# The plain split inputs of two feed-forwards begin at other bytes of on-chip memory

## The chip, the cores and the metric

The program runs on one NeuronCore of a Trainium2 chip. The metric is the device time of one execution in microseconds (us), the median of several. All arrays are float32.

## The reference

Four sub-layers over 256 tokens of width 2048: a gated DeltaNet mixer, a feed-forward, an HGRN2 mixer, a feed-forward. Each begins with an RMS norm and ends with a residual addition.

```python
def swiglu(h, w_gate, w_up, w_down):
    return (jax.nn.silu(h @ w_gate) * (h @ w_up)) @ w_down
...
    h = x
    for layer in range(DEPTH):            # DEPTH = 2
        if layer % 2 == 0:
            h = h + gdn_mixer(rmsnorm(h, gdn_norm[j]), gdn_w_in[j], ...)
        else:
            h = h + hgrn2_mixer(rmsnorm(h, hgrn_norm[j]), hgrn_w_in[j], ...)
        h = h + swiglu(rmsnorm(h, ffn_norm[layer]), w_gate[layer], w_up[layer], w_down[layer])
    return rmsnorm(h, final_norm)
```

The hidden width of a feed-forward is 5632, 22 groups of 256 (`N_FF`).

## The kernel before

**Split products.** A float32 operand is split into a high half (what TensorE's `float32r` form keeps) and a low half (the rest). A product is three matmuls: high by high, high by low, low by high. The input of a sub-layer is kept transposed, 128 features on the partitions and 256 tokens along the row, as `xt_h` (high) and `xt_l` (low): four tiles each, 4 blocks of 128 features in a tile, 1,024 bytes a block and partition. Weights come from memory as `raw` (or `sraw`), 1,024 columns at a time; ScalarE writes their high half `wh`, VectorE the low half `wl`.

**Two kinds of matmul.** A matmul has a stationary operand of 128 columns, loaded ahead by a weight load, and a moving one that streams past it. In the mixers' query, key and forget projections the weights are stationary and `xt` moves, 256 columns (`mm_cols`). Everywhere else (`mm_rows`) `xt`, or `ht` or `ot` of the output products, is stationary and the weights move, 512 columns; in the profile such a matmul reads `main<-wh,xt_h`: the moving operand stands first, the stationary one second.

**The feed-forward.** Of the 11 pairs of groups in each, four (`FF_PLAN`: those ahead of a colon) are computed by a seven-product scheme for 2 by 2 block matrices (`mixed_group`). Its products take 256 moving columns and write to `aux`. For products 1, 2 and 4 the stationary operand is a plain half of `xt`; for 3, 5, 6 and 7 it is a sum of blocks of the input, made once per feed-forward by `mix_inputs` into `mixh` and `mixl`. One step of a mixed group is four items: 6 matmuls of product 1; 12 of products 2 and 3 in turn; 12 of 5 and 7; 12 of 6 and 4. There are 4 such steps in a group, 8 mixed groups in a feed-forward. `among` puts the items between items of plain groups, or of the output product (`down`), 12 matmuls of 512 columns each. The other groups are plain: `xt` stationary, 512 moving columns.

**Where operands begin.** Tiles are laid out in the order of their pools. Some have columns to spare (`PAD`), and `make` picks where the data begins. All bytes here are modulo 512, within a partition. Moving weights begin at byte 32, stationary weights (in `mm_cols`) at 108 (`wh`) and 364 (`wl`). `mixh` begins at 108 and `mixl` at 364 (19 columns past 32 and 288). The eight `xt` tiles, `ht` and `ot` begin at 32. Every block of 128 columns is 512 bytes, so all blocks of an operand begin at the same byte modulo 512.

**The order.** The kernel records all operations and a planner then puts them in order, by costs and due times (`Recorder.plan`); matmuls of the main stream keep the order in which they were written. The next sub-layer's `xt` is made by `make_xt`, called by `next_input` for each quarter of the output product as that is finished.

Of the kernel before, what the change touches and what calls it, by code (L numbers as in the profile page):

```python
# [9 lines left out]
F32R = mybir.dt.float32r  # L10
# [7 lines left out]
P = 128  # L18
T = 256
# [60 lines left out]


PAD = 64
IN_COLS = {"wh": 108, "wl": 364}


class Op:
    __slots__ = ("eng", "method", "args", "kw", "cost", "lag", "main", "pred", "succ", "n", "late", "call", "tiles", "heirs", "share")

    def __init__(self, eng, method, args, kw, cost=0.0, lag=0.0, main=False):
        self.eng, self.method, self.args, self.kw = eng, method, args, kw  # L90
        self.cost, self.lag, self.main = cost, lag, main
        self.pred, self.succ = {}, []
        self.call, self.tiles, self.heirs = None, [], []
        self.share = 1.0


class Virtual:


    def __init__(self, pool, shape, dt, tag, bufs, name, stream=False):  # L100
        self.pool, self.shape, self.dt, self.tag, self.bufs, self.name = pool, list(shape), dt, tag, bufs, name
        self.stream = stream
        self.pad = self.cols = 0
        self.row = int(np.prod(shape[1:]))
        self.nbytes = self.row * (1 if dt == U8 else 4)
        self.touched = []
        self.before, self.ordered = None, False
        self.left = 0
        self.free = 0.0
        self.together = [self]  # L110
        self.slot = self.real = None
# [43 lines left out]
class Recorder:  # L155
# [38 lines left out]

    def after(self, ap):

        self.wanted = [other for other, *_ in self.virtual(ap).touched]

    def together(self, *aps):
        group = [self.virtual(ap) for ap in aps]  # L200
# [251 lines left out]
    def make(self, v):  # L452
        shape = [v.shape[0], v.shape[1] + v.pad] if v.pad else v.shape
        v.real = v.pool.real.tile(shape, v.dt, tag=f"{v.tag}.{v.slot}", name=v.name)
        assert v.real.offset == 0
        if v.pad:
            n = v.pool.padded.setdefault((v.tag, v.slot), len(v.pool.padded))
            at = 32 + n * v.pad * 4 % 512
            want = IN_COLS[v.tag] if v.cols else 32 + n % 2 * 512
            v.skip = (want - at) // 4  # L460
            assert 0 <= v.skip <= v.pad
# [61 lines left out]
class Trunk:  # L523
# [40 lines left out]
    def opening(self, items, setup):  # L564
        first = items[0].begin

        def begin():
            setup()
            first()

        items[0].begin = begin
        return items
# [3 lines left out]
    def setup(self):  # L576
        nc, c = self.nc, self.const
        t = lambda shape, tag, dt=F32: self.tile(c, shape, tag, dt)
        self.x_home = self.tile(self.dram, [T, D], "x_home", bufs=1)
        self.x_at, self.x = self.a["x"], {}  # L580
        neghalf = t([P, 72], "neghalf")
        self.neghalf = neghalf[:, 0:8]
        self.rstd = t([P, 2], "rstd")
        self.rstdh = t([P, 2], "rstdh")
        self.ssp = t([P, 2, 4], "ssp")
        self.ss = t([P, 2], "ss")
        head = t([P, P + 64], "head")
        nc.sync.dma_start(head, self.a["head"])
        nc.ops[-1].lag = 2.4
        self.queue = [nc.ops[-1]]  # L590
        self.ident = head[:, 0:P]
        self.norms = head[:, P : P + 64].rearrange("p (n c) -> p n c", n=4)
        self.ones = t([P, P], "ones")
        nc.gpsimd.memset(self.ones, 1.0)
        self.rstd_row = t([P, T], "rstd_row")
        self.junk = t([P, 512], "junk")
        self.vjunk = t([P, 320], "vjunk")[:, 0:256]
        nc.gpsimd.memset(self.neghalf, -0.5)
        self.xt_h = [t([P, 4, T], f"xt_h{i}", F32R) for i in range(4)]
        self.xt_l = [t([P, 4, T], f"xt_l{i}", F32R) for i in range(4)]  # L600

    def start(self, norm, row):

# [25 lines left out]
    def stream(self, items):  # L629
# [3 lines left out]
        def place(tag, cols):  # L633
            w = self.tile(self.wsplit, [P, 1024], tag, F32R, ordered=True)
            v = nc.virtual(w)
            v.pad, v.cols = PAD, cols
            return w
# [154 lines left out]
        if cg == 3:  # L792
            self.x_at = self.x_home

    def next_input(self, norm, row):


        def after(cg):
            self.make_xt(cg, norm)
            self.sumsq(cg)  # L800
            if cg == 3:
                self.make_rstd(row)

        return after
# [27 lines left out]
    def mix_inputs(self):  # L832
# [6 lines left out]
        self.mixed = [[], [], [], []]  # L839
        both = [self.tile(self.pool, [P, 4096 + PAD], f"mix{x}", F32R)[:, 19 : 19 + 4096] for x in "hl"]  # L840
        row = self.rstd_row.unsqueeze(1).broadcast_to([P, 4, T])
        for q in range(2):
# [16 lines left out]
            for n in range(4):  # L859
# [6 lines left out]
                self.mixed[n].append((h, low))  # L866

    def ffn(self, j, after):
        nc, a = self.nc, self.a
        hts, h1s, quick = {}, {}, {}  # L870
# [172 lines left out]
        def down(part, cg, pairs):  # L1043
            w = a[f"ffn_d{j}_{part}"]
            lo = sum(FF_PARTS[:part]) // 2

            def operand(kt):
                h, l = hts[pairs[kt // 4]]
                return h[:, kt % 4, :], l[:, kt % 4, :]

            last = part == len(FF_PARTS) - 1
            apart = last and j == 1 and cg == 3

            def end(ps):
                if apart:
                    self.finish_last(ps)
                    return
                self.add_x(ps, cg, not (last and j == 1))
                if last:
                    after(cg)  # L1060

            mm = self.mm_apart if apart else self.mm_rows
            n = len(pairs)
            return self.group(
                [w[cg, p - lo] for p in pairs],
                lambda ps, i, h, l: mm(ps, i, h, l, n, operand), end,
                lambda: self.load_x(cg), apart,
            )
# [425 lines left out]
    def gdn_o(self, hg, st):  # L1494
# [37 lines left out]
        st["ot"] = self.head_out(o, st["zs"], scale, self.gdn_hn)  # L1532

    def gdn(self, after):
        a = self.a
        states = [{} for _ in range(N_HG)]
# [41 lines left out]
    def out_proj(self, name, p, states, last, after):  # L1578
        two = states[2 * p : 2 * p + 2]

        def begin(cg):
            self.load_x(cg)

        def operand(kt):
            h, l = two[kt // 4]["ot"]
            return h[:, kt % 4, :], l[:, kt % 4, :]

        def make(cg):
            def end(ps):
                self.add_x(ps, cg)  # L1590
                if last:
                    after(cg)

            return self.group(
                [self.a[name][p, cg, i] for i in range(2)],
                lambda ps, i, h, l: self.mm_rows(ps, i, h, l, 2, operand), end,
                lambda: begin(cg),
            )

        return [item for cg in range(4) for item in make(cg)]  # L1600
# [260 lines left out]
    def finish(self, cg):  # L1861
        nc = self.nc
        if cg == 0:
            self.last = self.tile(self.pool, [P, 4096 + PAD], "mixl", F32R, ordered=True).bitcast(F32)[:, 0:D]
            nc.gpsimd.dma_start(self.last, self.a["final_norm"].broadcast_to([P, D]))
            self.y = self.tile(self.pool, [P, 4096 + PAD], "mixh", F32R, ordered=True).bitcast(F32)[:, 0:4096].rearrange("p (t c) -> p t c", t=2)
            self.part = self.tile(self.pool, [P, 2], "part")
# [43 lines left out]
    def run(self):  # L1911
        self.setup()
        self.start(0, True)
        items = self.gdn(self.next_input(1, True))
        items += self.ffn(0, self.next_input(2, True))
        items += self.hgrn(self.next_input(3, True))
        items += self.ffn(1, self.finish)
        self.stream(items)
        self.leave()
# [91 lines left out]
```

## Time and profile before

| | us |
|---|---|
| time before, median of 3 (lowest to highest) | 2740.96 (2739.41 to 2741.87) |
| profiled execution, its own time | 2739.51 |
| its span, first to last instruction | 2737.7 |
| DeltaNet mixer, about | 0 to 824 |
| first feed-forward, about | 824 to 1534 |
| HGRN2 mixer, about | 1534 to 2020 |
| second feed-forward, about | 2020 to 2727 |

PE is TensorE's matmuls, PEld its weight loads, DVE VectorE, ACT ScalarE. All instructions are issued from one helper line, so groups are told apart by the names of their tiles and by their sizes. The listed duration of a matmul contains its way through the array and overlaps the next one; the time from one start to the next tells what a matmul costs in a stream.

### The profile page before, as it was taken

The numbers are of one execution on the slowest core, as the hardware profiler recorded it, in microseconds if no ns is written. First come the engines' busy times: TensorE is split into PE (matmuls) and PEld (weight loads), VectorE is DVE, ScalarE is ACT, GpSimd is POOL, SyncE is SP. The second block draws the span as 40 slices with busy tenths as digits, with TensorE's granted clock in tenths as the row PEclk, the third lists the DMA queues.
The fourth block names the chain that finished last, engine by engine and source line by source line (L and its number), as shares of the span: only waits on it lengthen the run. The fifth ranks groups of instructions, "written<-read, shape, count | busy, mean of one in ns | idle before, by whom it ended". The sixth has DMA issues, their size and how long they took to land.

```text
span 2737.7 us, 44285 instructions
## 1 busy us (share of the span) xinstructions
PE 2719.8 (99%) x16822; PEld 2355.8 (86%) x16822; DVE 2168.5 (79%) x3309; ACT 1549.2 (57%) x2192; POOL 307.6 (11%) x466
## 2 busy tenths in 40 slices
PE   9999999999999999999999999999999999999998
PEld 9888888888888888888888989988888888888887
DVE  7787888877768898889867688778678898888665
ACT  6646666565555555555545556556465555555543
POOL 1213222232110000000010100000100000000000
PEclk9999999999999999999999999999999999999999
DMA  7686568686676667766676755545676667666764
GB/s 262 202 282 224 183 217 279 215 277 220 220 252 224 219 212 245 238 216 216 228 235 217 228 167 182 170 166 179 224 264 212 217 223 239 223 230 221 250 209 167
DMA packets 170376, 605.92 MB, mean 221 GB/s; under 512 B 21675, under 2 KB 22843, under 8 KB 170033
## 3 DMA queue, kind: packets, MB, share of 16 engines
q1 hardware_dynamic: 138912, 503.15, 56.1%
q0 software_dynamic: 30960, 99.08, 11.3%
q8 instruction: 132, 2.16, 0.3%
q14 instruction: 84, 0.68, 0.1%
q10 hardware_dynamic: 288, 0.85, 0.1%
HBM read 563.10 MB, written 39.89 MB: 220 GB/s over the span
## 4 chain that ended last, share of the span: by engine, by line
PE 96%; DVE 2%; ACT 1%; issue 1%; POOLq 0%; POOL 0%; DVEq 0%; ACTq 0%
PE main L496 80%; PE aux L496 17%; DVE wl L496 1%; DVE turned L496 1%; ACT wh L496 0%; ACT dec L496 0%; DVE htl L496 0%; DVE sraw L496 0%; ACT xt_h L496 0%; DVE h L496 0%; DVE utmp L496 0%; DVE pre L496 0%; DVE u L496 0%; ACT mixh L496 0%; POOLq L2007 0%
## 5 line engine op out<-in xcount | busy, mean ns | idle before, releaser
L496 ACT ACTIVATE wh<-raw 128x1024 fp32r<-128x1024 f32 x817 | 864.9, 1060 | 934.5 <-PE main L496 826.2
L496 DVE TENSOR_TENSOR wl<-raw,wh 128x1024 fp32r<-128x1024 f32 x817 | 1002.6, 1229 | 422.3 <-ACT wh L496 412.3
L496 PE MATMUL main<-wh,xt_h 128*128 128x512 f32 x1664 | 651.5, 391 | 0.8 <-ACT wh L496 0.8
L496 PE MATMUL main<-wl,xt_h 128*128 128x512 f32 x1664 | 650.7, 391 | 1.3 <-DVE wl L496 1.3
L496 PE MATMUL main<-wh,xt_l 128*128 128x512 f32 x1664 | 650.3, 391 | 0.0
L496 PEld LDWEIGHTS main<-wh,xt_l 128*128 128x128 f32 x1664 | 312.5, 188 | 65.1
L496 PEld LDWEIGHTS main<-wh,xt_h 128*128 128x128 f32 x1664 | 312.7, 188 | 62.8 <-ACT wh L496 1.2
L496 PEld LDWEIGHTS main<-wl,xt_h 128*128 128x128 f32 x1664 | 312.6, 188 | 61.7 <-DVE wl L496 1.6
L496 ACT ACTIVATE wh<-sraw 128x1024 fp32r<-128x1024 f32 (+1 forms) x256 | 243.4, 951 | 136.7 <-PE main L496 96.3
L496 DVE TENSOR_TENSOR wl<-sraw,wh 128x1024 fp32r<-128x1024 f32 (+1 forms) x256 | 278.3, 1087 | 27.1 <-ACT wh L496 25.0
L496 PE MATMUL main<-xt_h,wh 128*128 128x256 f32 (+1 forms) x1040 | 288.7, 278 | 0.7 <-ACT wh L496 0.7
L496 PE MATMUL main<-xt_h,wl 128*128 128x256 f32 (+1 forms) x1040 | 288.3, 277 | 1.1 <-DVE wl L496 0.9
L496 PE MATMUL main<-xt_l,wh 128*128 128x256 f32 (+1 forms) x1040 | 288.2, 277 | 0.3 <-DVE xt_l L496 0.3
L496 PE MATMUL main<-wh,hth 128*128 128x512 f32 x680 | 266.5, 392 | 1.0 <-ACT hth L496 1.0
L496 PE MATMUL main<-wl,hth 128*128 128x512 f32 x680 | 266.2, 391 | 0.0
L496 PE MATMUL main<-wh,htl 128*128 128x512 f32 x680 | 265.2, 390 | 0.4
L496 PEld LDWEIGHTS main<-xt_h,wl 128*128 128x128 f32 (+1 forms) x1040 | 194.4, 187 | 1.6 <-DVE wl L496 1.5
L496 PEld LDWEIGHTS main<-xt_h,wh 128*128 128x128 f32 (+1 forms) x1040 | 194.5, 187 | 1.3 <-ACT wh L496 0.9
L496 PEld LDWEIGHTS main<-xt_l,wh 128*128 128x128 f32 (+1 forms) x1040 | 194.5, 187 | 1.0 <-DVE xt_l L496 0.5
L496 PEld LDWEIGHTS main<-wh,htl 128*128 128x128 f32 x680 | 127.7, 188 | 29.2 <-DVE htl L496 1.7
L496 PE MATMUL main<-wh,ot_l 128*128 128x512 f32 x384 | 151.3, 394 | 0.0
L496 PE MATMUL main<-wh,ot_h 128*128 128x512 f32 x384 | 150.5, 392 | 0.0
(238 smaller groups left out, 4078.5 us busy)
## 6 DMA issues: line engine op xcount, KB each, us to landing
raw<-in_ffn_gu SPq DMA_DIRECT2D x224, 512.0 KB, 4.7
raw<-in_ffn_d SPq DMA_DIRECT2D x176, 512.0 KB, 4.7
sraw<-in_ffn_gu SPq DMA_DIRECT2D x128, 512.0 KB, 5.2
raw<-in_hgrn_in SPq DMA_DIRECT2D x128, 512.0 KB, 4.1
raw<-in_gdn_kq SPq DMA_DIRECT2D x64, 512.0 KB, 5.3
raw<-in_gdn_v SPq DMA_DIRECT2D x64, 512.0 KB, 4.8
raw<-in_gdn_z SPq DMA_DIRECT2D x64, 512.0 KB, 4.9
raw<-in_gdn_out SPq DMA_DIRECT2D x64, 512.0 KB, 5.1
```

Source lines behind the costliest of these rows:

```text
L496: getattr(getattr(tc.nc, op.eng), op.method)(*args, **kw)
```

## The change

The four high tiles become one tile of 4,096 columns and 24 to spare, the four low ones one tile of 4,096 columns and 104 to spare. A new pair is declared ahead of each sub-layer (`new_xt`), in the same memory, with its own beginning: byte 32 for both halves in the mixers ("rows"), byte 108 (high) and 364 (low) in the feed-forwards ("mixed"). Together the tiles are 512 bytes longer than before, so that whatever lies behind them keeps its byte modulo 512. `after`, which orders the sums of squares behind the writes of one quarter, now looks at the quarter's region instead of at its tile. On every engine the instructions, their order and the places where they wait are the same as before; only addresses differ.

```diff
+XT_PAD = {"h": 24, "l": 104}
+XT_SKIP = {"rows": {"h": 0, "l": 104}, "mixed": {"h": 19, "l": 59}}
...
     def after(self, ap):
-        self.wanted = [other for other, *_ in self.virtual(ap).touched]
+        v = self.virtual(ap)
+        p0, p1, f0, f1 = v.region(ap)
+        self.wanted = [
+            other for other, _, (a0, a1, b0, b1) in v.touched if a0 < p1 and p0 < a1 and b0 < f1 and f0 < b1
+        ]
...
-        if v.pad:
+        if v.pad and v.skip is None:
...
-        self.xt_h = [t([P, 4, T], f"xt_h{i}", F32R) for i in range(4)]
-        self.xt_l = [t([P, 4, T], f"xt_l{i}", F32R) for i in range(4)]
+        self.new_xt("rows")
+
+    def new_xt(self, kind):
+        both = []
+        for half in "hl":
+            t = self.tile(self.const, [P, 16 * T], f"xt_{half}", F32R, ordered=True)
+            v = self.nc.virtual(t)
+            v.pad, v.skip = XT_PAD[half], XT_SKIP[kind][half]
+            t = t.rearrange("p (g k t) -> p g k t", g=4, k=4)
+            both.append([t[:, cg] for cg in range(4)])
+        self.xt_h, self.xt_l = both
...
-    def next_input(self, norm, row):
+    def next_input(self, norm, row, kind):
         def after(cg):
+            if cg == 0:
+                self.new_xt(kind)
             self.make_xt(cg, norm)
...
-        items = self.gdn(self.next_input(1, True))
-        items += self.ffn(0, self.next_input(2, True))
-        items += self.hgrn(self.next_input(3, True))
+        items = self.gdn(self.next_input(1, True, "mixed"))
+        items += self.ffn(0, self.next_input(2, True, "rows"))
+        items += self.hgrn(self.next_input(3, True, "mixed"))
```

More of the change, by code (lines that the diff above doesn't have):

```diff
@@ L103, in __init__ @@
         self.pad = self.cols = 0
+        self.skip = None
         self.row = int(np.prod(shape[1:]))
```

## The prediction

> **What bounds the kernel now.** I read the page first (the span, the engines' shares, the chain that ended last), then the windows of the two feed-forwards, the waits there, and last single matmuls in the timeline. From the page:
>
> ```profile
> span 2737.7 us, 44285 instructions
> PE 2719.8 (99%) x16822; PEld 2355.8 (86%) x16822; DVE 2168.5 (79%) x3309; ACT 1549.2 (57%) x2192; POOL 307.6 (11%) x466
> PE 96%; DVE 2%; ACT 1%; issue 1%; POOLq 0%; POOL 0%; DVEq 0%; ACTq 0%
> ```
>
> The chain is PE for 96% of the span. Next the two feed-forwards by windows (stretch, its length, then busy time and count of PE, PEld, DVE, ACT, POOL, granted clock, DMA share, GB/s), and PE's waits in the first of them:
>
> ```profile
> 823.70:1533.90 710.20, 709.50 (x3782) 611.96 (x3781) 580.35 (x749) 378.49 (x442) 40.19 (x65) 1.00 0.69 226
> 2019.90:2727.30 707.40, 706.69 (x3758) 609.44 (x3756) 576.86 (x742) 373.07 (x430) 38.36 (x63) 1.00 0.68 221
> PE main L496 <- ACT hth L496: 0.5, 2, 0.3
> ```
>
> PE is busy all but 0.7 us of each and waits 0.5 us in all of the first; DVE, the next fullest, is at 580 of 710. So a feed-forward lasts as long as its matmuls take from start to start, and a nanosecond off a matmul there is a nanosecond off the program until DVE, with 18% to spare, comes due. The granted clock is full.
>
> What the change touches is the stationary `xt` of the feed-forwards. How many matmuls that is, by the windows of `xt_h` and of `xt_l` alone (first the two of `xt_h`, then of `xt_l`), and the groups of 256 moving columns, with the count over both feed-forwards and the mean ns of one:
>
> ```profile
> 823.70:1533.90 710.20, 351.45 (x1280) 227.46 (x1281) 11.58 (x20) 6.32 (x16) 1.00 0.69 226
> 2019.90:2727.30 707.40, 351.31 (x1280) 227.40 (x1280) 6.65 (x8) 1.66 (x4) 1.00 0.68 221
> 823.70:1533.90 710.20, 228.48 (x640) 120.75 (x640) 11.58 (x20) 1.00 0.69 226
> 2019.90:2727.30 707.40, 228.48 (x640) 120.77 (x640) 6.65 (x8) 1.00 0.68 221
> ...
> L496 PE MATMUL aux<-wl,mixh 128*128 128x256 f32 x512 | 142.8, 279 | 0.0
> L496 PE MATMUL aux<-wl,xt_h 128*128 128x256 f32 x384 | 108.6, 283 | 0.0
> L496 PE MATMUL main<-wh,xt_h 128*128 128x512 f32 x1664 | 651.5, 391 | 0.8 <-ACT wh L496 0.8
> ```
>
> Each feed-forward has 1280 + 640 = 1920 matmuls on `xt`, 3840 in both. Of these 3 x 384 = 1152 have 256 moving columns (one group of three is shown) and 3840 - 1152 = 2688 have 512. The mixed sums make 3 x 512 = 1536 more of 256. Same shape, same moving weights at byte 32: with `mixh` (byte 108) one takes 279 ns in the mean, with `xt_h` (byte 32) 283. The last row has the 512-column ones of all stages, 391. Durations overlap, so the price is read from starts. One whole step of a mixed group in the timeline (start us, us, then the instruction), four items and the 512-column matmuls behind the first:
>
> ```profile
> 910.75 0.39 PE L496 MATMUL main<-wh,xt_l 128*128 128x512 f32 x1
> 910.98 0.28 PE L496 MATMUL aux<-wh,xt_h 128*128 128x256 f32 x1
> 911.10 0.28 PE L496 MATMUL aux<-wl,xt_h 128*128 128x256 f32 x1
> ...
> 911.58 0.28 PE L496 MATMUL aux<-wh,xt_l 128*128 128x256 f32 x1
> 911.70 0.40 PE L496 MATMUL main<-wh,xt_h 128*128 128x512 f32 x1
> ...
> 913.08 0.39 PE L496 MATMUL main<-wh,xt_h 128*128 128x512 f32 x1
> ...
> 914.44 0.28 PE L496 MATMUL aux<-wh,xt_h 128*128 128x256 f32 x1
> ...
> 915.85 0.40 PE L496 MATMUL main<-wh,xt_h 128*128 128x512 f32 x1
> ...
> 918.60 0.28 PE L496 MATMUL aux<-wh,mixh 128*128 128x256 f32 x1
> ...
> 918.95 0.28 PE L496 MATMUL aux<-wh,mixh 128*128 128x256 f32 x1
> ...
> 919.97 0.40 PE L496 MATMUL main<-wh,xt_h 128*128 128x512 f32 x1
> ...
> 922.72 0.28 PE L496 MATMUL aux<-wh,mixh 128*128 128x256 f32 x1
> ...
> 924.13 0.40 PE L496 MATMUL main<-wh,xt_h 128*128 128x512 f32 x1
> ```
>
> Read the starts. Five matmuls on `xt`, from 911.10 to 911.70, take 0.60 us: 120 ns each. The third item has sums alone; its last nine, 918.95 to 919.97, take 1.02: 113.3 ns each. The first three of that item take 0.35, 117 each: behind matmuls on byte 32 it needs three to reach its pace. For 512 columns the price differs: 913.08 to 914.44 is six in 1.36, 226.7 ns each, which is just twice 113.3 although the stationary `xt` begins at byte 32; only the first six behind a 256-column item, 911.70 to 913.08, take 1.38.
>
> **The change part by part.** *The 1152 plain matmuls of 256 columns.* They get the bytes that the sums have. The four items last 0.72, 1.41, 1.37 and 1.41 us by their starts, 4.91 for 6 + 12 + 12 + 12 = 42 matmuls; at 113.3 each they would last 4.76. The step is worth 0.15 us, and there are 2 x 8 x 4 = 64 of them (64 x 18 = 1152, as counted): 9.6 us. Not all of that need go. The entry behind 512-column matmuls costs 0.35 - 0.34 = 0.01 us an item, four items a step, 256 in all: up to 3 us stay if it outlives the change, as it must behind `ht`, which stays at byte 32. So 6.6 to 9.6 us come off.
>
> *The 2688 plain matmuls of 512 columns.* No row shows one with its stationary operand at 108 or 364. The nearest: at byte 32 they already run at twice the pace of the best 256-column matmuls, so there is little to win in the steady stream: nothing, but for the first six behind an item, 0.02 us a block of 12; with at most 2 x 64 blocks of plain groups beside mixed ones (32 items for each of two mixed pairs), 0 to 2.6 us. What can be lost is bounded by the price that a bad byte has at 256 columns, 120 - 113.3 = 6.7 ns a load: 2688 x 6.7 ns = 18.0 us. I take no loss, since the load covers at most the first half of a 512-column stream, and in the 256-column stream beside moving weights at byte 32 a load from 108 or 364 costs nothing visible. But both ends stay in the range, for what a load disturbs may depend on the length of the stream.
>
> *Writing and reading `xt` elsewhere.* Per feed-forward 16 ACT and 16 DVE writes and four DVE sums touch the new bytes. The nearest rows, a low half at byte 364 against one at 32, and a high half at 108 against one at 32, 512 elements each (ACT's second row reads `sraw`):
>
> ```profile
> L496 DVE TENSOR_TENSOR mixl<-h,mixh 128x512 fp32r<-128x512 f32 x16 | 10.8, 688 | 0.4 <-ACT mixh L496 0.4
> L496 DVE TENSOR_TENSOR wl<-sraw,wh 128x512 fp32r<-128x512 f32 x64 | 43.9, 686 | 3.7 <-ACT wh L496 3.5
> L496 ACT ACTIVATE mixh<-h 128x512 fp32r<-128x512 f32 x16 | 9.5, 619 | 1.3 <-DVE h L496 1.3
> L496 ACT ACTIVATE wh<-sraw 128x512 fp32r<-128x512 f32 x64 | 40.5, 633 | 34.5 <-PE main L496 17.6 <-PE aux L496 15.2 <-DVE wl L496 1.7
> ```
>
> 688 against 686 ns, 619 against 633: some 72 instructions at 2 ns or so are 0.1 us. Nothing. The new dependence (one tile for four, so that the first write waits for the last reader of the whole old tile) is free: the old input's last reader stands before the output product whose first finished quarter calls for the write. Without that cover it would cost a stall of PE at three places, and the order shows none.
>
> *The sum.* 6.6 to 9.6 and 0 to 2.6: between 6.6 and 12.2 us off; I take 8.8, the entry surviving behind `ht` and half of the rest. The profiled execution of 2739.51 would become 2730.7; it lay 1.4 under the median, so against the median 2740.96 I say 2732.2.
>
> **A rule against it.** The trace first: equal shapes, the same moving operand, 120 ns against 113.3. The Trainium skill ("TensorE: Matmul & The Clock Gate", step-by-step part of "What happens when you issue a matmul") says that the stationary and the moving operand have read ports of their own, so that a load takes nothing from the running matmul; by that rule no byte would matter and the change would be worth nothing. The 6.7 ns are against it wherever a load fills the stream, at 256 columns; at 512 columns the steady 226.7 ns agree with it.
>
> **The rivals.** *The long matmuls pay.* A load from 108 or 364 disturbs the 512-column stream as one from 32 disturbs the 256-column one. The place is the plain groups of both feed-forwards, the price 6.7 ns each: +18.0 - 8.8 = 9 us slower, 2750; without the 256-column gain behind them (each item again entering from a bad pace) up to 2753. For it: the entry rows, where three loads from 108 and 364 behind 512-column matmuls cost 117 instead of 113.3, so that there is a state of the stream in which these bytes are the bad ones. Against it: the state is gone after three. It decides from 8.8 / 2688 = 3.3 ns a matmul, and slower by over 0.2% (5.5 us, about what a measurement of this kernel can tell from no change) from 5.3 ns.
>
> *They pay in part.* The stream falls into the bad state, leaves it after a few matmuls as in the entry, and falls back. At 1.5 to 3.7 ns in the mean (up to the entry's 117 - 113.3), 4 to 10 us are lost against 8.8 won: 2736 to 2742, within 0.2%.
>
> *The byte is not the cause.* `xt` and the sums also lie in different parts of memory, and no row shows a full stationary operand at byte 32 under 256 moving columns anywhere else. If the place matters and not the byte, nothing changes: 2741. Against it: the sums themselves go at 117 behind operands at byte 32 and at 113.3 behind their own kind, so that more than their place decides. This is also where the rule of the separate ports would end.
>
> **How the numbers follow.** Forecast (short ones gain, long ones unhurt) 0.42; long ones pay in full 0.31; in part 0.19; no effect 0.08. The forecast alone has 2728 to 2735; the lowest is 2740.96 - 12.2 = 2729, and 1 more if long matmuls gain at their pace. With the other cases the range runs to 2751, near the top of the second case; beyond it lie fewer than 1 in 10. Faster by over 0.2%: 0.42; within 0.2%: the part and no-effect cases, 0.27; slower: 0.31.
>
> **What would show it.** Right: the `aux` matmuls on `xt` at 276 to 279 ns instead of 283, steps of 42 near 4.78 us instead of 4.91, six plain matmuls in 1.36 us throughout, each feed-forward 4 to 5 us shorter, the mixers unchanged. Wrong: plain 512-column matmuls at 230 ns or more from start to start in the middle of a plain group, or their mean duration above 391 ns; then the feed-forwards grow where the mixed pairs are not. If the short ones stay at 120, the byte was not the cause.

## The result and the profile after

| | us, median | runs |
|---|---|---|
| before | 2739.83 (2739.19 to 2741.87) | 6 |
| after | 2751.10 (2749.78 to 2752.29) | 6 |

The change makes the kernel 11.3 us slower: ratio 1.0040, 95% interval 1.0027 to 1.0052. That is the first rival, not the forecast. All times of this document are of runs at the full granted clock; one run of the later kernel `pair` had a granted clock of 0.58, took 4606 us and is left out.

From the page of after, the span, the engines and the chain by engine:

```profile
span 2750.6 us, 44285 instructions
PE 2731.1 (99%) x16822; PEld 2353.9 (86%) x16822; DVE 2169.5 (79%) x3309; ACT 1549.2 (56%) x2192; POOL 307.0 (11%) x466
PE 96%; DVE 2%; issue 1%; ACT 1%; DMA 1%; SPq 0%; POOLq 0%; POOL 0%; DVEq 0%; ACTq 0%
```

PE is still the chain. DVE and ACT have the busy time of before (2168.5, 1549.2), so writing and reading `xt` at its new place costs nothing. The two feed-forwards of after by windows (columns as in the prediction):

```profile
826.30:1541.60 715.30, 714.50 (x3782) 610.48 (x3781) 580.59 (x749) 378.30 (x442) 40.30 (x65) 1.00 0.68 225
2027.60:2740.20 712.60, 711.80 (x3758) 607.97 (x3756) 577.42 (x742) 372.83 (x430) 38.50 (x63) 1.00 0.67 220
```

Each is 5.1 to 5.2 us longer than before, at full clock, with PE idle for 0.8 us (0.7 before): the matmuls themselves take longer. That is 10.3 of the 11.3 us; the rest is within the interval. The HGRN2 mixer between them lasts 486.0 us in both. The 2.6 us by which the first feed-forward starts later (826.3 against 823.7) are not shown to be part of the effect. Counted by the feed-forward's first long matmul on `xt` it starts at 823.9 before and 826.5 after, and in the profiled executions of the 14 kernels below anywhere from 824.0 to 826.3; the latest, `pair192`, has all that lies ahead of it as in the kernel before.

Groups by form in after; the mean ns is the second number behind the bar. Before they were 279, 283, 391 and, for `hth`, 392:

```profile
L503 PE MATMUL aux<-wl,mixh 128*128 128x256 f32 x512 | 142.1, 277 | 0.0
L503 PE MATMUL aux<-wl,xt_h 128*128 128x256 f32 x384 | 106.8, 278 | 0.0
L503 PE MATMUL main<-wh,xt_h 128*128 128x512 f32 x1664 | 654.9, 394 | 0.8 <-ACT wh L503 0.8
L503 PE MATMUL main<-wh,hth 128*128 128x512 f32 x680 | 266.5, 392 | 1.2 <-ACT hth L503 1.2
```

By their mean durations the short ones came down as foretold, the long ones on `xt` lost 3 ns in a mean over all four stages, and those on `ht`, which stayed at byte 32, lost nothing. The price shows in the starts. A step of the timeline of after (start us, us, instruction):

```profile
915.19 0.28 PE L503 MATMUL aux<-wh,xt_h 128*128 128x256 f32 x1
...
915.90 0.39 PE L503 MATMUL main<-wh,xt_h 128*128 128x512 f32 x1
...
917.06 0.39 PE L503 MATMUL main<-wh,xt_l 128*128 128x512 f32 x1
917.29 0.40 PE L503 MATMUL main<-wh,xt_h 128*128 128x512 f32 x1
917.53 0.40 PE L503 MATMUL main<-wl,xt_h 128*128 128x512 f32 x1
917.76 0.39 PE L503 MATMUL main<-wh,xt_l 128*128 128x512 f32 x1
917.99 0.39 PE L503 MATMUL main<-wh,xt_h 128*128 128x512 f32 x1
...
918.70 0.28 PE L503 MATMUL aux<-wh,xt_h 128*128 128x256 f32 x1
...
922.88 0.28 PE L503 MATMUL aux<-wh,mixh 128*128 128x256 f32 x1
...
923.59 0.28 PE L503 MATMUL aux<-wh,mixh 128*128 128x256 f32 x1
...
924.27 0.39 PE L503 MATMUL main<-wh,xt_h 128*128 128x512 f32 x1
```

Twelve long ones, 915.90 to 918.70, take 2.80 us, 233.3 each; before, settled, 2.72. The starts from 917.06 to 917.99 lie 0.23, 0.24, 0.23, 0.23 apart: by the unrounded records the stream repeats 231, 231, 236, 236 ns. The item of six short ones, 915.19 to 915.90, takes 0.71 (by the unrounded records 0.712, and 0.713 before). Of the item of sums alone the first six take 0.71, 118.5 each, and only the last six, 923.59 to 924.27, go at 113.3. Behind long matmuls on `ht` the entry is shorter. An item of six there, and the matmul that follows it:

```profile
1016.83 0.28 PE L503 MATMUL aux<-wh,xt_h 128*128 128x256 f32 x1
...
1017.53 0.40 PE L503 MATMUL main<-wh,hth 128*128 128x512 f32 x1
```

0.70 us (0.694 by the records) instead of 0.71. How settled the price of the long ones is, by a stretch of 85 us inside the longest unbroken run of them, 384 in a row; the count behind PE's busy time tells the pace (one or two of each count began before the stretch). Before, then after:

```profile
1380.00:1465.00 85.00, 85.00 (x377) 70.41 (x376) 52.05 (x68) 38.06 (x42) 6.96 (x12) 1.00 0.73 233
1385.00:1470.00 85.00, 85.00 (x366) 68.78 (x365) 51.15 (x67) 37.09 (x41) 6.97 (x12) 1.00 0.72 228
```

From first to last start the run takes 86.81 us before and 89.37 after, 383 steps: 226.7 and 233.3 ns. The loss does not wear off within it. By the sum of all times from start to start, by kind, in the first feed-forward (the second is alike to 0.7 us), with two kernels of the experiments:

| us | before | after | all32 | pair224 |
|---|---|---|---|---|
| 1344 long on `xt` | 306.2 | 313.5 | 306.3 | 304.8 |
| 1056 long on `ht` | 242.4 | 242.5 | 242.3 | 241.0 |
| 576 short on `xt` | 69.3 | 67.5 | 69.5 | 68.7 |
| 768 short, sums | 88.7 | 88.3 | 91.7 | 90.5 |

Before to after: +7.3 +0.1 -1.8 -0.4, to 0.1 us the +5.1 of its window.

### The profile page after: what moved, and what is told of

Same layout as the page of the kernel before. It is cut to its first block, busy times and chain, and to the rows that moved or that the text cites. A ratio compares the mean times of both kernels' runs of the same rounds, so it can differ in the third digit from the quotient of the medians.

```text
span 2750.6 us, 44285 instructions
## 1 busy us (share of the span) xinstructions
PE 2731.1 (99%) x16822; PEld 2353.9 (86%) x16822; DVE 2169.5 (79%) x3309; ACT 1549.2 (56%) x2192; POOL 307.0 (11%) x466
## 3 DMA queue, kind: packets, MB, share of 16 engines
q0 software_dynamic: 30960, 99.08, 11.3%
## 4 chain that ended last, share of the span: by engine, by line
PE 96%; DVE 2%; issue 1%; ACT 1%; DMA 1%; SPq 0%; POOLq 0%; POOL 0%; DVEq 0%; ACTq 0%
PE main L503 79%; PE aux L503 16%; DVE wl L503 1%; DVE turned L503 1%; DMA raw<-in_gdn_z 0%; DMA first<-in_x 0%; ACT wh L503 0%; ACT dec L503 0%; DVE htl L503 0%; DVE sraw L503 0%; DVE h L503 0%; DVE utmp L503 0%; DVE pre L503 0%; SPq L503 0%; ACT xt_h L503 0%
```

## The experiments

The theory after the result: a load that begins at another byte than the moving operand disturbs the long stream and helps the short one, by the distance between the two. The rivals: it is the new form (one tile for four, other dependences), or the bytes 108 and 364 by themselves.

**bytes32: the new form with the old bytes.**

```diff
-XT_SKIP = {"rows": {"h": 0, "l": 104}, "mixed": {"h": 19, "l": 59}}
+XT_SKIP = {"rows": {"h": 0, "l": 104}, "mixed": {"h": 0, "l": 104}}
```

> The changed kernel with one edit: in the feed-forwards both halves of xt begin at byte 32 again; the two long tiles, their spare columns and the new order of dependences stay. If the bytes made the loss, the time is that of before, 2740 within 3 us, and the plain 512-column matmuls of the feed-forwards go at 226.7 ns from start to start. If the new form of the tiles made it, 2751 stays.

2740.13 us (10 runs), ratio 0.9999 (0.9990 to 1.0009). Its first feed-forward by windows:

```profile
824.20:1534.40 710.20, 709.49 (x3782) 611.92 (x3781) 580.08 (x749) 378.52 (x442) 40.18 (x65) 1.00 0.69 226
```

That is the 710.2 of before to a tenth, so the form and its dependences cost nothing, and the whole loss is the byte's.

**halves: one half at a new byte.** High halves at 108 in the first feed-forward, low halves at 364 in the second, the others at 32.

```diff
-XT_SKIP = {"rows": {"h": 0, "l": 104}, "mixed": {"h": 19, "l": 59}}
+XT_SKIP = {"rows": {"h": 0, "l": 104}, "high": {"h": 19, "l": 104}, "low": {"h": 0, "l": 59}}
...
```

> The changed kernel, in the first feed-forward with the high half of xt at 108 and the low half at 32, in the second with the high half at 32 and the low half at 364. If each load pays for its own byte, the 512-column matmuls of the first go at about 226.7 + 2/3 x 6.7 = 231 ns in the mean, of the second at 226.7 + 1/3 x 6.7 = 229. If one load at a wrong byte throws the stream out for several matmuls, both go at 232 or more.

2749.82 us (one run). 85 us inside the run of 384, first and second feed-forward:

```profile
1384.00:1469.00 85.00, 85.00 (x369) 69.22 (x368) 51.74 (x67) 37.10 (x41) 6.97 (x12) 1.00 0.72 229
2585.00:2670.00 85.00, 85.00 (x369) 68.94 (x368) 51.59 (x67) 36.86 (x41) 6.98 (x12) 1.00 0.73 236
```

Both settle at 231.1 ns, and not the moved loads alone: in the run of 384 of the first, matmuls with their stationary operand at 32 and at 108 take 231.0 and 231.2 in the mean from start to start. One odd load in three slows its neighbours by two thirds of the full price here; in the second feed-forward's unbroken run of 154 long matmuls it costs all of it, 233.3 settled.

**Four kernels that sweep the byte**, the moving weights at 32, the low halves 256 bytes behind the high ones. The edit, with the number of skipped elements for each byte (byte = 32 + 4 x skip):

```diff
-XT_PAD = {"h": 24, "l": 104}
+XT_PAD = {"h": 64, "l": 64}
-XT_SKIP = {"rows": {"h": 0, "l": 104}, "mixed": {"h": 19, "l": 59}}
+XT_SKIP = {"rows": {"h": 0, "l": 64}, "first": {"h": 16, "l": 16}, "second": {"h": 32, "l": 32}}
...
```

> The plain stationary operands begin at bytes 96 and 352 (high, low halves) in the first feed-forward and at 160 and 416 in the second; the sums stay at 108 and 364, the moving weights at 32. All four bytes are 32 modulo 64, which 108 and 364 (44 modulo 64) are not. Theory A (only the place modulo 64 counts): as at byte 32, long matmuls 226.7 to 227.7 ns from start to start, plain short ones 118.9, feed-forwards 710.2 and 707.4 us. Theory B (only the same byte modulo 512, or modulo 256, counts as equal): as with the change, long 233.2 and short 115.5, feed-forwards 715.3 and 712.6. Theory C (the distance to the moving operand counts, in steps of 64 modulo 512): as B in at least one feed-forward, with different numbers in the two.

> The same with bytes 64 and 320 in the first feed-forward, 48 and 304 in the second: 0 and 48 modulo 64. Theory A: neither is 32 modulo 64, so both pay as with the change, long 233.2 ns, short 115.5. Theory D (what counts is that the operand begins at a multiple of 16 or 32 bytes, which 108 and 364 do not): bytes 64 and 320 go like byte 32 (long 226.7 to 227.7, short 118.9); 48 and 304 too if the multiple is 16, but like the change if it is 32. Theory B: both like the change.

> The same with bytes 36 and 292 in the first feed-forward, 40 and 296 in the second: 4 and 8 bytes past the moving operand's byte 32. Theory A, B and D alike: long 233.2 ns and short 115.5 in both, feed-forwards about 715 and 712.5 us. Theory E (the distance has to be some ten bytes or more before the two operands part): both as at byte 32, long 226.7 to 227.7, short 118.9.

> The same with bytes 32 and 288 in the first feed-forward (only the low halves move, by 256) and 236 and 492 in the second (44 modulo 64, as 108 and 364 are). Theory A: first feed-forward 710.2 us with long 227.7 ns and short 118.9, second 712.6 with long 233.2 and short 115.5. Theory B with 512: the first pays as well, since a single wrong load in three did (long 231 ns, about 714 us); with 256 it does not. For the second all of them say about 712.6, unless the place modulo 256 counts by itself, then long ones come out between 226.7 and 233.

2751.20, 2753.95, 2752.53 and 2750.76 us (one run each; before beside them 2741.62). 85 us inside the runs of 384, in the order 96, 160, 64, 48, 36, 40, 32 with 288, 236:

```profile
1383.00:1468.00 85.00, 85.00 (x366) 68.48 (x365) 51.15 (x67) 36.64 (x40) 6.98 (x12) 1.00 0.71 227
2586.00:2671.00 85.00, 85.00 (x367) 68.92 (x366) 51.48 (x67) 36.74 (x41) 6.98 (x12) 1.00 0.73 235
1387.00:1472.00 85.00, 85.00 (x365) 68.40 (x365) 51.14 (x66) 36.44 (x40) 6.97 (x12) 1.00 0.72 227
2591.00:2676.00 85.00, 85.00 (x377) 70.38 (x376) 52.04 (x68) 37.83 (x42) 6.98 (x12) 1.00 0.75 238
1387.00:1472.00 85.00, 85.00 (x367) 68.61 (x366) 51.47 (x67) 37.09 (x41) 6.95 (x12) 1.00 0.72 228
2588.00:2673.00 85.00, 85.00 (x370) 69.25 (x369) 51.47 (x67) 36.91 (x42) 6.96 (x12) 1.00 0.73 236
1382.00:1467.00 85.00, 85.00 (x377) 70.38 (x376) 51.96 (x68) 37.87 (x42) 6.97 (x12) 1.00 0.73 232
2585.00:2670.00 85.00, 85.00 (x362) 68.02 (x362) 50.43 (x66) 36.44 (x39) 6.88 (x12) 1.00 0.71 232
```

| bytes | settled long, ns | short plain, mean ns to the next short one | feed-forward, us |
|---|---|---|---|
| 96, 352 | 233.3 | 115.5 | 714.7 |
| 160, 416 | 232.4 | 119.1 | 714.0 |
| 64, 320 | 233.3 | 118.8 | 718.2 |
| 48, 304 | 226.7 here, 233.3 in the runs of 154 and 72 | 118.4 | 713.0 |
| 36, 292 | 232.4 | 118.0 | 717.5 |
| 40, 296 | 230.7 | 117.6 | 711.3 |
| 32, 288 | 226.7 | 118.8 | 710.2 |
| 236, 492 | 235.3 | 117.2 | 716.9 |

Only the pair that is equal to the moving byte modulo 256 keeps the long matmuls at 226.7 throughout; four bytes off is enough to lose. The place modulo 64 (96 and 160 are 32 modulo 64) does not save them. The short ones come down to 115.5 only at byte 96 here, 64 from the weights, and to 115.7 with the change (before: 118.8). At 48 there are two states: the same operands run at 226.7 in the run of 384 and at 233.3 in the shorter ones, so that something beside the two bytes counts too; what it is, no run shows. (The second feed-forward is 2.7 us shorter than the first in the kernel before.)

**moving, match, match64: the other operand.** If only the two bytes against each other counted, moving the weights would do the same, and moving both would undo it. In `moving` all moving weights of the feed-forwards begin at 212 and 468 (first) and 108 and 364 (second), `xt` and `ht` at 32, the sums at 108 and 364. In `match` and `match64` the weights and `xt` move together, to 108 and to 64 (first) and 48 (second), except that in the second feed-forward of `match` `xt` begins 76 bytes behind the weights, at 184; the low halves lie 256 further, `ht` stays.

```diff
-            want = IN_COLS[v.tag] if v.cols else 32 + n % 2 * 512
+            want = v.cols[v.tag] if v.cols else 32 + n % 2 * 512
...
+        for item in items + waiting:
+            item.cols = ({"wh": 212, "wl": 468}, {"wh": 108, "wl": 364})[j]
```

> The kernel before, with xt at byte 32 and the sums at 108/364; only the moving weights of the feed-forwards begin elsewhere, at 212 (high) and 468 (low) in the first, at 108 and 364 in the second. Modulo 256 the stationary xt then begins 76 bytes past the moving operand in the first feed-forward, as it does in the changed kernel, and 76 short of it in the second. If the distance between the two decides: first feed-forward, xt with 256 columns at 113.3 ns and with 512 columns at 233; second, sums with 256 columns (distance 0) at 120. If the stationary byte alone decides, all is as before: 120 and 226.7 on xt, 113.3 on the sums, in both.

> In the feed-forwards the moving weights begin at 108 (high) and 364 (low). The plain stationary operands begin at 108 and 364 in the first feed-forward, so that both operands have the same byte modulo 256, and at 184 and 440 in the second, 76 behind the moving ones as with the change. The hidden operands stay at 32, so they are unequal throughout. If it is equality modulo 256 that counts, the long plain matmuls of the first feed-forward run at 226.7 ns in the middle of a plain group, although their byte is the one that cost 233.3 with the change, and the short ones and sums at 120. If byte 108 is bad by itself, the first feed-forward keeps 233. If the distance alone counts, the second has 233.3 for the long plain ones and some 115.5 for the short ones; if the moving operand's own byte counts too, it has other numbers.

> As the kernel with equal bytes at 108, but the moving weights and the plain stationary operands of the feed-forwards begin together at 64 and 320 in the first, and together at 48 and 304 in the second; the sums stay at 108 and 364, the hidden operands at 32. If equal bytes were only worth 227.5 to 231 ns at 108 because 108 is not a multiple of 32, the long plain matmuls run at 226.7 to 227.7 at 64; at 48 they do too if a multiple of 16 is enough, otherwise some of the three products of a group keep 228 to 231. If byte 32 is good by itself, whatever the other operand does, both cost 231 or more. Short plain ones at 120 in both by the rule of equal bytes.

2773.65, 2752.06 and 2756.99 us (one run each). 85 us inside the runs of 384, first and second feed-forward of `moving`, of `match`, and of `match64`:

```profile
1404.00:1489.00 85.00, 85.00 (x359) 67.75 (x358) 50.46 (x66) 36.11 (x41) 6.98 (x12) 1.00 0.71 222
2609.00:2694.00 85.00, 85.00 (x374) 69.97 (x373) 52.02 (x67) 37.80 (x42) 6.98 (x12) 1.00 0.75 240
```

```profile
1385.00:1470.00 85.00, 85.00 (x373) 69.60 (x372) 51.24 (x67) 37.50 (x40) 6.90 (x12) 1.00 0.73 229
2587.00:2672.00 85.00, 85.00 (x369) 69.39 (x368) 51.37 (x67) 36.81 (x41) 6.98 (x12) 1.00 0.72 234
```

```profile
1386.00:1471.00 85.00, 85.00 (x377) 70.38 (x376) 51.92 (x67) 37.46 (x40) 6.75 (x12) 1.00 0.74 232
2592.00:2677.00 85.00, 85.00 (x371) 69.23 (x370) 50.80 (x67) 37.52 (x40) 6.74 (x12) 1.00 0.73 235
```

`moving` fells the distance as the whole story. A stationary operand at 32 beside weights at 212 begins 76 behind them modulo 256, as one at 108 beside weights at 32 does, but the long ones settle at 237.8 ns instead of 233.3, and the short ones have 121 to 122, and the first feed-forward lasts 739.3 us; with the weights at 108 the long ones pay little, 228.3. `match` shows that equality helps but is not all: at 108 the long ones settle at 228.9 (231.0, 227.3 and 228.3 for the three products), nearer to 226.7 than to 233.3; its short ones, equal too, have 119 to 120. In its second feed-forward the same distance as with the change, 76, gives 231.1, not 233.3. `match64` settles what was left: both operands at 64, a multiple of 32, run at 226.75 although 64 against 32 had cost 233.3, while both at 48 run at 230.0 in the run of 384, 231.1 in those of 72 and 233.3 in that of 154, and the long ones on `ht`, now unequal at 32 against 64, pay 233.3. So byte 32 is not good and 108 not bad by itself. Long matmuls keep their pace throughout where both operands begin at the same byte modulo 256 and at a multiple of 32; that is what 32, 288 and 64, 320 share and 48 and 108 lack. It is the simplest rule that fits these four places, and no fifth was tried. For the short ones the rule of equal bytes missed: 120 ns was expected in both feed-forwards, and their mean is 118.

**pair, all32, pair64, pair224, pair192: short and long ones with different bytes.** The short matmuls come in items of their own weights, so that the weights' byte can differ there while all stationary operands stay at 32 and the long ones stay equal. In `pair` the items with short products have their weights at 212 and 468, in `all32` nothing but the sums moves (to 32).

```diff
-        both = [self.tile(self.pool, [P, 4096 + PAD], f"mix{x}", F32R)[:, 19 : 19 + 4096] for x in "hl"]
+        both = [self.tile(self.pool, [P, 4096 + PAD], f"mix{x}", F32R)[:, at : at + 4096] for x, at in (("h", 0), ("l", 64))]
...
+        for item in items:
+            if item.ring:
+                item.cols = {"wh": 212, "wl": 468}
```

> The kernel before, with all stationary operands of the feed-forwards at byte 32, the sums too, and the moving weights of the mixed items alone at 212 (high) and 468 (low): distance 76 modulo 256 for the 256-column matmuls, distance 0 for the 512-column ones. If the distance decides, the short ones go at 113.3 and the long ones at 226.7, and the time is 6 to 10 us under before, 2730 to 2734: faster than both kernels. If the stationary byte decides, all 2688 short ones go at 120: 2750.

2744.67 us (10 runs), ratio 1.0015 (1.0006 to 1.0024): a miss. The short ones run at 116 to 124 ns, the sums at 119.6 in the mean against 115.5 before.

> The kernel before, with the sums too at byte 32 (the low halves at 288, equal modulo 256). If equality is the good case for long and the bad one for short matmuls, all 1344 short ones of a feed-forward run at 120 ns: the sums lose 768 x 4.6 = 3.5 us; and no long one pays behind an item: 1344 x 1.0 = 1.3 us and 1056 x 1.5 = 1.6 us come back. About 710.8 us for the first feed-forward. If the long ones pay behind any switch of length, whatever the bytes, they stay at 227.7 and 228.3 and it is 713.6.

2747.97 us (one run), its first feed-forward:

```profile
826.00:1539.30 713.30, 712.77 (x3782) 615.15 (x3781) 580.33 (x749) 378.54 (x442) 40.19 (x65) 1.00 0.69 225
```

The table above has its parts. The sums lose 3.0 us, as short matmuls on equal bytes do, but the long ones win nothing back: behind an item they take 233, 236, 228, 233, 231 before they settle, as before. So that entry does not come from unequal operands. The bytes of the short items do count in it: in `pair` only the first two pay (233, 231 ns).

> The kernel before, with all stationary operands of the feed-forwards at 32 modulo 256, the sums too; only the moving weights of the items with 256-column products go elsewhere: to 224 and 480 in the first feed-forward (stationary 64 behind them, the distance of 96 to 32 that gave 115.6 ns) and 96 and 352 in the second (64 ahead of them). Long matmuls stay equal modulo 256. If the distance alone counts, the first feed-forward has its 1344 short matmuls at about 115 and long ones at 226.7 to 227.1: 576 x 3.4 = 2.0 us and 1344 x 0.8 = 1.1 us less, 707.5 us instead of 710.2; both feed-forwards so: about 2735.5. If the moving operand's own byte counts, as with 212 and 468, the short ones take 117 to 121 and it comes out at 2741 to 2745.

2740.50 us (11 runs), ratio 1.0001 (0.9992 to 1.0010). The two feed-forwards differ: 708.4 us with the weights at 224 and 480 (before: 710.2), 710.1 at 96 and 352 (before: 707.4). Neither distance gave 115: 117.5 to 117.9 ns at 224. What is better there is the long ones.

> The kernel before, with all stationary operands of the feed-forwards at 32 modulo 256 (the sums too) and the moving weights of the items with 256-column products at 224 and 480 in both feed-forwards. In the first feed-forward this gave 708.4 us instead of 710.2. If the byte decides and not the stage, the second gives 1.7 us as well, 705.7 instead of 707.4, and the whole 2736.4 against 2739.8: ratio 0.9988. If a feed-forward's 1.7 us were chance, no difference.

2736.85 us (2736.02 to 2738.65, 11 runs) against 2740.17 (15 runs beside it): ratio 0.9988, 0.9979 to 0.9997, as expected to half a microsecond. It is the only kernel here that is faster than both, by 0.12% of the kernel before. Its feed-forwards, and long matmuls behind an item of six in its timeline:

```profile
824.60:1533.00 708.40, 707.68 (x3782) 612.48 (x3780) 580.31 (x748) 378.56 (x442) 40.19 (x65) 1.00 0.69 227
2019.00:2724.70 705.70, 704.98 (x3758) 610.06 (x3756) 577.00 (x742) 372.97 (x430) 38.36 (x63) 1.00 0.68 222
```

```profile
911.69 0.28 PE L496 MATMUL aux<-wh,xt_h 128*128 128x256 f32 x1
...
912.40 0.39 PE L496 MATMUL main<-wh,xt_h 128*128 128x512 f32 x1
...
913.76 0.39 PE L496 MATMUL main<-wh,xt_h 128*128 128x512 f32 x1
...
915.12 0.28 PE L496 MATMUL aux<-wh,xt_h 128*128 128x256 f32 x1
```

The first six long ones behind the item take 1.36 us, 912.40 to 913.76, as the next six do; in the kernel before the first six take 1.38. By the table the gain is 1.4 + 1.4 us on long matmuls and 0.6 on short plain ones, less 1.8 lost on the sums: 1.7 us a feed-forward, and not the gain that the prediction counted on.

> The same with the moving weights of those items at 192 and 448 in the first feed-forward and 160 and 416 in the second, all multiples of 32, 96 and 128 from the stationary operand. If any multiple of 32 that is far enough away does as 224, both have the short ones at 117.6 ns and the long ones at 226.7, 708.4 and 705.7 us. If the place counts in finer ways, as 96 and 352 (118.1, 228.1 ns, 710.1 us) already say, one of them is worse than 224, or better.

2748.95 us (one run): 712.1 us with 192 and 448, 712.6 with 160 and 416, both worse than before. The short ones take some 119 ns, and the long ones pay at the entry again. 224 is a find, not a rule.

## Why the prediction was wrong

**What bounds the kernel: right.** PE alone; DVE and ACT unchanged; each nanosecond of a matmul shows in the end. The HGRN2 mixer did not change, and the new dependence and the writes cost nothing (`bytes32`, and the busy times of after).

**The step that failed: the 2688 long matmuls, "I take no loss".** They lost 7.3 us in each feed-forward, 14.5 in all, 5.4 ns each in the mean, against the 3.3 from which the rival decided. The sign of being wrong that the prediction names, 230 ns or more in the middle of a plain group, is there: 233.3. The upper bound, 6.7 ns a load or 18.0 us, is the settled price to the tenth (89.37 - 86.81 us over 383 steps). That is luck as far as these runs show: the bound was taken from the short matmuls, where the unequal pair is the faster one, and other unequal pairs cost the long ones 1.7 to 11.1 ns. The mean is lower because the long ones before already paid behind each item (233, 236, 228, 233, 230 ns), while the first behind an item in after takes 226. The reason given was that a load covers at most half of a long stream. The weight loads of before, on long matmuls and on short ones of sums:

```profile
L496 PEld LDWEIGHTS main<-wh,xt_h 128*128 128x128 f32 x1664 | 312.7, 188 | 62.8 <-ACT wh L496 1.2
L496 PEld LDWEIGHTS aux<-wh,mixh 128*128 128x128 f32 x512 | 96.9, 189 | 4.3
```

A load is on record for 188 or 189 ns at both lengths, though the short ones, with a load each, start every 113.3 ns. So the record contains the load's way, as with the matmuls, and the stream gives a load no more than 113.3 ns, half of 226.7. That premise stands; what failed is the step from it to no loss. A load that fits into half of a long stream can slow that stream all the same, by 6.7 ns here. The other half of the reason, that beside moving weights at 32 a load from 108 "costs nothing visible" in the short stream, carried a property of one length over to another with the opposite sign: equal bytes are the bad case for the short ones (120 against 113.3) and the good one for the long ones (226.7 against 233.3).

**The term that was mis-sized: the 1152 short matmuls.** 6.6 to 9.6 us were forecast with up to 3 for the entry; measured were 1.8 or 1.9 on plain ones and 0.4 on sums a feed-forward, 4.6 in all by the unrounded records. Behind `ht` the items went as forecast (0.694 us for six, 3 matmuls of entry). Behind long matmuls on `xt` at the new bytes the entry became six matmuls at 116 to 122, so that an item of six, at 0.712 us against 0.713, gained nothing, and an item of sums alone lost 0.02 us (1.374 to 1.392). The first rival had this ("each item again entering from a bad pace"); it was right in sign and place. That its 2750 is within 1.1 us of 2751.1 is partly luck: it has 3.5 us too much loss on the long ones and 4.2 us too much gain on the short ones, and the two errors offset each other. Nor is it the load's byte alone, as it says, but the byte against that of the weights (`moving`, `match64`). The second rival, a stream that leaves the bad state again, fell with the run of 384, and the third, place instead of byte, with `bytes32`.

**The rule of separate ports.** "TensorE: Matmul & The Clock Gate" of the Trainium skill (step-by-step part of "What happens when you issue a matmul") says that loading the next weights takes no read bandwidth from the running matmul. By that rule, as the prediction read it, every byte is equal. The prediction let the settled 226.7 ns at 512 columns stand for it; byte 36 against byte 32, at 232.4 ns, speaks against that reading there too. The trace decides: which two bytes the operands begin at changes the pace at both lengths.

**Open.** Why equal and unequal act in opposite ways on the two lengths, what entry a switch of length has, why 224 frees it, and why 48 has several paces, was measured and not explained. No run moved the stationary `ht` or varied the length itself.

## What to carry to other kernels

Where matmuls run back to back, read their price from start to start, for each length and for each pair of start bytes apart; a byte that is good for one length can be the bad one for the other, and there may be more of the other. Before an operand that two kinds of matmul share is moved, multiply the largest price seen for any kind by the count of the most numerous kind, and let that bound weigh as much as the gain. What one can change without touching the numerous kind (here the weights of the short items alone) is the place to try first, and to try at several bytes.

## What the hardware showed that was not expected

- float32r matmuls with 128 stationary and 512 moving columns, back to back, settle at 226.7 ns if both operands begin at the same byte modulo 256 and at a multiple of 32 (32, 288, 64 and 320 seen), else at 228.3 to 237.8 in these runs, with one stream at 226.7 against that (48 against 32). Equal bytes at 48 give 230.0 to 233.3.
- One differing load in three slows the whole stream (231.1 ns, in one run of matmuls 233.3).
- With 256 moving columns equal bytes settle at 120 (32 and 108 seen; 64 and 48 have 118 in the mean), and stationary operands at 96 or 108 beside weights at 32 at 113.3; the others have 117 to 122 in the mean.
- The pace of a stream depends on the stream before it: the same short item takes 0.694 us behind an undisturbed long stream and 0.712 behind a disturbed one, and the same long matmuls take 1.38 us for the first six behind one kind of short item and 1.36 behind another.
